# Last layer's experts in seven groups of two and three, and the first group's weights fetched while the mixer still runs

## The chip, the cores and the metric

The kernel runs on one core of one Trainium2 chip. The metric is the device time of one launch in microseconds (us). Three launches of the kernel before took 1733.53, 1736.21 and 1737.06 us; the median, 1736.21 us, is the time before.

## The reference, cut to what matters

The program is a two-layer transformer block followed by a second, different block. Only the end of the first block's last layer matters here: a retention mixer over 512 tokens, a residual, and then a mixture of experts over the last 256 tokens. All is float32.

```python
y, yc = retention_mixer(xm, cm, ret_w_in[idx], ret_w_out[idx], ...)
h = h + g1 * y
xm2 = modulate(rmsnorm(h, norm_g[layer, 1]), sh2, sc2)
f = moe_ffn(xm2.reshape(-1, D), router_w, router_b, moe_w1[layer], moe_w3[layer], moe_w2[layer])
h = h + g2 * f.reshape(h.shape)
...
def moe_ffn(tok, router_w, router_b, w1, w3, w2):
    ...
    for e in range(N_EXPERTS):
        hid = jax.nn.silu(tok @ w1[e]) * (tok @ w3[e])
        out = out + gate[:, e:e + 1] * (hid @ w2[e])
    return out
```

There are 16 experts, each token goes to 2 of them, D is 1024 and the hidden width of an expert is 512. So w1, w3 and w2 of one expert hold 2 MiB each, and all experts of a layer 96 MiB.

## The kernel before, in words

**How the experts are computed.** The kernel doesn't run every token through every expert. It gives each expert a fixed number of rows (a cap) in a group of 128 rows, gathers the chosen tokens into these rows by matmuls with a 0/1 matrix (`gather`, L1382), runs the group through the weights of its experts (`products`, L1403), scales the rows by their gates into `y` (ACT L1451 and DVE L1452) and scatters them back into the accumulator `acc` by matmuls (`scatter`, L1409). `GROUPS[1]` lists the groups of the last layer; `BATCHES` says which groups share one gather. Experts 15 and 14 have fixed places; the fourteen others are ranked on the chip by how many tokens they got, and `(0, 96)` stands for the expert of rank 0 with 96 rows. Where an expert has more tokens than rows, a slow path behind a branch (`overflow`, L1546 to L1548) does the rest.

**What a group costs.** For the 128 rows of a group, `products` makes 24 steps of 512 columns: eight for w1, eight for w3, eight for w2 (four parts of the hidden width, two halves of the output). With several experts in a group the rows are split into column tiles (two of 64, or four of 32) that TensorE works on side by side; each tile reads its own expert's weights.

**How the weights come.** `expert_load` (L192 through `raw`) fetches a piece of 1 MiB, half a matrix, with one DMA on SP's queue; an expert has six pieces, in the order w1, w1, w3, w3, w2, w2. `raw` takes the slots of `self.slots` in turn. `moe_late`, the function of this stage, opens eight slots on the right side of SBUF beside the three that the whole program keeps (`RAW = 3`), so eleven pieces of 8 KiB per partition fit at once. SP works in order: a load whose slot is still being read waits, and all later loads wait behind it. Loads of ranked experts read the expert's number from SBUF first (`values_load` in `places_of`). For the first two groups (`NS = 2`) the loads are issued ahead of the routing (`first`).

**What runs ahead.** `mixer1` is the retention mixer. Its activations `x` (`xact`, 32 KiB per partition) are read by `project(h)` for four heads; `attend(h)` then works on what `project` left in the pool `l1w`. The output projection (`out_T`, eight loads of `ret_w_out`) is interleaved with `attend(3)` and follows it. POOL computes the `rstd` powers (L502) of `attend` in order with its other work.

**Order.** The Tile scheduler sets each engine's order from the code's order, priorities and the pools' releases; a tile in a freed pool waits for the last reader of what lay there.

Of the kernel before, what the change touches and what calls it, by code (L numbers as in the profile page):

```python
# [9 lines left out]
F32 = mybir.dt.float32  # L10
# [8 lines left out]
P = 128  # L19
# [19 lines left out]
NS = 2  # L39
one, two = lambda r: ((r, 128),), lambda a, b: ((a, 64), (b, 64))  # L40
SPLIT = (0, 2, 4, 7, 10, 12)
GROUPS = ((one(15), one(14), one(0), two(8, 13), one(1), one(2), two(9, 12), one(3), one(4), two(10, 11), one(5),
           one(6), one(7)),
          (one(15), one(14), ((0, 96), (13, 32)), ((1, 96), (12, 32)), two(2, 11), two(3, 10), two(4, 9), two(5, 8),
           two(6, 7)))
BATCHES = ((0, 1), (2, 3), (4, 5), (6, 7), (8,))
CAPS = [[dict(x for g in gs for x in g)[r] for r in range(16)] for gs in GROUPS]


# [81 lines left out]
class Kern:  # L131
    def __init__(self, tc, ctx, I, out):
        self.tc, self.nc, self.I, self.out, self.ctx = tc, tc.nc, I, out, ctx
        self.cp = ctx.enter_context(tc.tile_pool(name="const", bufs=1))
        self.sm = ctx.enter_context(tc.tile_pool(name="small", bufs=3))
        self.ps = ctx.enter_context(tc.tile_pool(name="psum", bufs=4, space=PSUM))
        self.nid = 0
        self.aside, self.work = [], []
        self.holds, self.added, self.added_to = [], None, None
        self.slots, self.turn = [], 0  # L140
        ctx.enter_context(self.buffers(RAW))


# [25 lines left out]
    @contextmanager  # L169
    def buffers(self, n, **kw):  # L170

        with self.pool(self.name("raw"), n, **kw) as pool:
            old = self.slots
            self.slots = old + [pool] * n
            yield
            self.slots = old

    @contextmanager
    def splitting(self):
# [390 lines left out]
    def mixer0(self):  # L570
        nc, I, V = self.nc, self.I, self.nc.vector
        W = I["mixab_w_in"][0]
        with ExitStack() as es:
# [147 lines left out]

            Wo, Y = I["mixab_w_out"][0], [[self.psum(tag="g") for _ in range(2)] for _ in range(2)]

            def out_T(c):
                return self.part_T_steps(Y[c], Wo, 0, 256 * c, mx, 0, 512, True, True, (0, 1, 2, 3, 4, 5, 6, 7))

# [7 lines left out]
            for c in range(4):  # L734
                if c > 1:
                    Y.append([self.psum(tag="g") for _ in range(2)])
                    ys.append(out_T(c))
# [48 lines left out]
    def mixer1(self, ss):  # L786
        nc, I, V = self.nc, self.I, self.nc.vector
        W, Wo = I["ret_w_in"][0], I["ret_w_out"][0]
        with ExitStack() as es:
            op = lambda n, b: es.enter_context(self.pool(n, b))  # L790
            lp, wp = op("l1", 1), op("l1w", 2)
            rb = self.stat_end(ss, 0, 512)
            x = self.xact(lp)
            for k in range(KC):
                self.mod_norm(1, rb, x, k)
                self.fill(FT[8 + k])
# [106 lines left out]
            for h in range(3):  # L903
                self.work = [project(h + 1)]
                attend(h)
                self.step(999)
            self.fill(99)
            Y = [self.psum((P, 2, 256), "g") for _ in range(4)]
            self.work = [out_T(0, c) for c in range(4)]
            attend(3)  # L910
            self.step(999)
            for c in range(4):
                self.work = [out_T(8, c)]
                self.step(999)
                if c == 0:
                    ss = self.stat_begin(self.router_begin(1))
                if c == 1:
                    self.router_shift(1)
                for j in range(2):
                    self.residual(1, 2, 2 * c + j, Y[c][:, j], 256)  # L920
                    self.stat_chunk(ss, 2 * c + j, 256, 256)
        return ss


    def router_begin(self, l):
# [362 lines left out]
    def moe_late(self, ss):  # L1288
# [3 lines left out]
        l, n0, NT, N = 1, 256, 2, 256  # L1292
        with ExitStack() as es:
            op = lambda n, b=1: es.enter_context(self.pool(f"{n}{l}", b))
            es.enter_context(self.buffers(8, side="right"))
            rp, wp = op("route"), op("moe", 2)
            order, GR = {}, GROUPS[l]
            load = lambda *a: self.expert_load(l, order, *a)

            def loads(g):  # L1300

                rs = [r for r, _ in GR[g]]
                return [[load(name, r, u, n, c) for r in rs]
                        for name, n, c in (("moe_w1", 8, 512), ("moe_w3", 8, 512), ("moe_w2", 4, 1024)) for u in range(2)]

            first = [loads(g) for g in range(NS)]
            tl, places, gates, rows, nat = self.route(l, ss, rp)
            self.holds = []
            pos, posm = places()
# [18 lines left out]

            cur = batch(BATCHES[0])
            pm, oi, ranked = self.ranking(tl, pos, NT, lambda: tl([NT, 16, 16]))  # L1330
            ranked(place, posm, V)
            rows()
            g, den = gates()
# [17 lines left out]
            def slots(g, oh, a):  # L1351

                ex = GR[g]
                sp = self.psum((P, 2, 4))
                for i, (r, _) in enumerate(ex):
                    for t in range(NT):
                        nc.tensor.matmul(sp[:, i], oh[:, t, a:a + P], pr4[:, r, t, :], start=t == 0, stop=t == NT - 1)
# [2 lines left out]
                for i, (r, n) in enumerate(ex):  # L1360
                    for b in range(a, a + n, 32):

                        c = b + (n if n in (64, 128) else 32)
# [50 lines left out]
            todo = None  # L1414
            for bi, gs in enumerate(BATCHES):
                x, oh, _ = cur
                nxt = batch(BATCHES[bi + 1]) if bi + 1 < len(BATCHES) else None
                chunks = list(range(4)) if nxt else []
                for i, g in enumerate(gs):
                    if g >= NS:  # L1420
                        self.places_of(order, oi, GR[g])
                    ws = loads(g) if g >= NS else first[g]
                    xs = lambda k: x[:, k, P * i:P * i + P]
                    h1 = self.psum()
                    products([h1], xs, ws[0:2], g)
# [28 lines left out]
                    todo = y, back  # L1454
# [622 lines left out]
```

## Time and profile before

| | |
|---|---|
| median of three launches | 1736.21 us |
| the profiled execution | 1734.04 us, span 1732.3 us |
| mean granted TensorE clock of it | 0.976 |
| busy: PE, DVE, ACT, POOL | 94%, 50%, 37%, 15% of the span |
| bytes over the DMA engines | 390 MB, mean 225 GB/s |
| last layer's experts, first to last `products` matmul | 1024.2 to 1280.9 us |

The profile comes from one execution; its own time is 2.2 us below the median of the launches. PE is TensorE's matmul, DVE VectorE, ACT ScalarE, POOL GpSimd; SP issues DMAs. Times in rows are microseconds from the span's start. A PE that is shown busy may still be waiting inside a matmul, so the rows of waits and of DMA traffic are read beside the busy time.

### The profile page before, as it was taken

The numbers are of one execution on the slowest core, as the hardware profiler recorded it, in microseconds if no ns is written. First come the engines' busy times: TensorE is split into PE (matmuls) and PEld (weight loads), VectorE is DVE, ScalarE is ACT, GpSimd is POOL, SyncE is SP. The second block draws the span as 40 slices with busy tenths as digits, with TensorE's granted clock in tenths as the row PEclk, the third lists the DMA queues.
The fourth block names the chain that finished last, engine by engine and source line by source line (L and its number), as shares of the span: only waits on it lengthen the run. The fifth ranks groups of instructions, "written<-read, shape, count | busy, mean of one in ns | idle before, by whom it ended". The sixth has DMA issues, their size and how long they took to land.

```text
span 1732.3 us, 26549 instructions
## 1 busy us (share of the span) xinstructions
PE 1636.9 (94%) x10640; PEld 1222.9 (71%) x10640; DVE 874.4 (50%) x1676; ACT 643.6 (37%) x1008; POOL 266.0 (15%) x265
## 2 busy tenths in 40 slices
PE   5999999988999998999999989999989999999999
PEld 3676657665555455879899955343449999999899
DVE  6565554573424346644555442111135756677665
ACT  3343333333423244433434331010135555655543
POOL 2212101221111111201211020000012110123300
PEclk8999999898999999999999989999989999999999
DMA  9644654477999987354433467999975454433360
GB/s 312 151 134 147 209 187 167 147 311 254 400 384 380 394 326 282 121 194 148 147 122 122 146 252 239 410 420 420 420 257 179 141 159 161 160 122 122 122 214 25
DMA packets 179230, 390.00 MB, mean 225 GB/s; under 512 B 25063, under 2 KB 141864, under 8 KB 149850
## 3 DMA queue, kind: packets, MB, share of 16 engines
q1 hardware_dynamic: 173882, 375.83, 60.1%
q0 software_dynamic: 4336, 10.99, 2.4%
q8 instruction: 87, 1.43, 0.3%
q10 hardware_dynamic: 880, 1.38, 0.2%
q14 instruction: 45, 0.37, 0.1%
HBM read 381.50 MB, written 14.85 MB: 229 GB/s over the span
## 4 chain that ended last, share of the span: by engine, by line
PE 66%; DVE 6%; issue 2%; ACT 2%; POOL 1%; DMA 1%; POOLq 0%; ACTq 0%; DVEq 0%
PE ps L220 12%; PE ps L221 12%; PE ps L222 12%; PE ps L1403 11%; PE ps L1174 8%; PE ps L280 3%; PE ps L1382 1%; DVE wl L211 1%; PE ps L1409 1%; DVE X L1956 1%; PE ps L408 1%; PE ps L1970 1%; DMA w<-in_moe_w_dram 1%; PE ps L1858 0%; PE ps L1839 0%
## 5 line engine op out<-in xcount | busy, mean ns | idle before, releaser
L211 DVE TENSOR_TENSOR wl<-w,wh 128x1024 fp32r<-128x1024 f32 x278 | 346.3, 1261 | 167.3 <-ACT wh L208 165.8
L208 ACT ACTIVATE wh<-w 128x1024 fp32r<-128x1024 f32 x280 | 290.9, 1056 | 200.2 <-PE ps L221 93.1
L220 PE MATMUL ps<-wh,xh 128*128 128x256 f32 x512 | 146.7, 286 | 1.6 <-DVE qk L553 1.6
L221 PE MATMUL ps<-wl,xh 128*128 128x256 f32 x512 | 144.8, 283 | 0.0
L222 PE MATMUL ps<-wh,xl 128*128 128x256 f32 x512 | 144.7, 283 | 0.0
L1403 PE MATMUL ps<-w,xe 128*64 128x512 f32 (+2 forms) x640 | 136.8, 595 | 0.0
L1174 PE MATMUL ps<-w,xe 128*64 128x512 f32 (+1 forms) x320 | 103.6, 596 | 1.2 <-DMA w<-in_moe_w_dram 1.2
L220 PE MATMUL ps<-x,wh 128*128 128x256 f32 x352 | 102.3, 291 | 0.0
L220 PEld LDWEIGHTS ps<-wh,xh 128*128 128x128 f32 x512 | 98.1, 192 | 5.7 <-issue 2.7
L221 PE MATMUL ps<-x,wh 128*128 128x256 f32 x352 | 99.8, 283 | 0.0
L222 PE MATMUL ps<-x,wl 128*128 128x256 f32 x352 | 99.8, 283 | 0.0
L221 PEld LDWEIGHTS ps<-wl,xh 128*128 128x128 f32 x512 | 98.2, 192 | 0.2
L222 PEld LDWEIGHTS ps<-wh,xl 128*128 128x128 f32 x512 | 98.2, 192 | 0.0
L1403 PEld LDWEIGHTS ps<-w,xe 128*64 128x64 f32 (+2 forms) x640 | 43.4, 131 | 72.9 <-issue 70.4
L220 PE MATMUL ps<-xh,wh 128*128 128x512 f32 (+1 forms) x224 | 83.2, 380 | 3.4 <-ACT xh L541 3.0
L221 PE MATMUL ps<-xl,wh 128*128 128x512 f32 (+1 forms) x224 | 82.7, 371 | 1.6 <-DVE xl L542 1.1
L222 PE MATMUL ps<-xh,wl 128*128 128x512 f32 (+1 forms) x224 | 81.4, 364 | 0.9 <-DVE wl L211 0.9
L1174 PEld LDWEIGHTS ps<-w,xe 128*64 128x64 f32 (+1 forms) x320 | 38.3, 158 | 57.5 <-issue 54.6
L220 PEld LDWEIGHTS ps<-x,wh 128*128 128x128 f32 x352 | 67.1, 191 | 1.4
L221 PEld LDWEIGHTS ps<-x,wh 128*128 128x128 f32 x352 | 67.3, 191 | 1.2 <-issue 0.2
L220 PE MATMUL ps<-wh,xp 128*128 128x256 f32 x224 | 65.5, 292 | 2.3 <-ACT xp L1659 2.3
L222 PEld LDWEIGHTS ps<-x,wl 128*128 128x128 f32 x352 | 67.2, 191 | 0.4
(472 smaller groups left out, 3669.8 us busy)
## 6 DMA issues: line engine op xcount, KB each, us to landing
w<-in_moe_w_dram SPq DMA_DIRECT2D x192, 1024.0 KB, 11.6
w<-in_w_in_dram SPq DMA_DIRECT2D x48, 1024.0 KB, 5.0
w<-in_ada_w_dram SPq DMA_DIRECT2D x40, 1024.0 KB, 5.1
w<-in_ret_w_in_dram SPq DMA_DIRECT2D x24, 1024.0 KB, 5.2
w<-in_mixab_w_in_dram SPq DMA_DIRECT2D x10, 1024.0 KB, 6.2
w<-in_ada_w_dram SPq DMA_DIRECT2D x16, 512.0 KB, 8.4
w<-in_ret_w_out_dram SPq DMA_DIRECT2D x8, 1024.0 KB, 5.1
w<-in_mixab_w_out_dram SPq DMA_DIRECT2D x4, 1024.0 KB, 7.4
```

Source lines behind the costliest of these rows:

```text
L208: nc.scalar.activation(hi, t[:, b:b + hk], AF.Copy)
L211: eng.tensor_tensor(out=lo, in0=t[:, b:b + hk], in1=hi.bitcast(F32), op=OP.subtract)
L220: mm(ps, lh, rh, start=start, stop=False, skip_group_check=skip)
L221: mm(ps, lh, rl, start=False, stop=False, skip_group_check=skip)
L222: mm(ps, ll, rh, start=False, stop=stop, skip_group_check=skip)
L280: self.nc.tensor.transpose(out, in_, self.ident[:n, :n])
L408: nc.tensor.matmul(ps[32 * j:32 * j + 32, :], self.S[:, kc, :], w[:, j * 512:(j + 1) * 512], start=kc == 0, stop=kc == KC - 1)
L1174: nc.tensor.matmul(ps[a], x[0][:, q, a], t[:, k, s], start=first, stop=last)
L1382: nc.tensor.matmul(ps[:, j, 0:w], nat[i % 2][:, i // 2, k * P:(k + 1) * P], oh[:, i // 2, 0:w], start=i == 0, stop=i == 2 * NT - 1)
L1403: nc.tensor.matmul(ps[a:b], lhs(u * m + k)[:, a:b], we[e][:, k, 512 * c:512 * c + 512], start=u == k == 0, stop=u == len(ws) - 1 and k == ...
L1409: nc.tensor.matmul(acc[k // 2][:, k % 2], y[i][:, k * P:(k + 1) * P], back, start=start and k % 2 == i == 0, stop=stop and i == 1, skip_gr ...
L1956: mul = lambda e, o, i1: e.tensor_tensor(out=o, in0=o, in1=i1, op=OP.mult)
```

## The change

The last layer gets seven groups in place of nine: experts 15 and 14 share one (64 rows each, 128 each before), rank 0 shares with rank 13 as before, ranks 1 and 2 have 64 rows each in groups of three with two experts of 32 rows, and ranks 3 to 8 are in pairs. The caps of ranks 9, 10 and 11 fall from 64 to 32, that of rank 1 from 96 to 64. The first group is a batch of its own.

The eight right-hand slots are no longer opened by `moe_late`. `x` of the mixer moves into a pool of its own on the right side, which is closed after `project(3)`; there `ahead(4, ...)` opens four slots and issues the four w1 pieces of experts 15 and 14 on POOL's queue. After `attend(3)` the pool `l1w` is closed and the four w3 pieces follow in the same way. `moe_late` takes these eight slots over (`joined`); of the first group only the four w2 pieces are left to SP, and all later groups load when their turn comes.

```diff
-          (one(15), one(14), ((0, 96), (13, 32)), ((1, 96), (12, 32)), two(2, 11), two(3, 10), two(4, 9), two(5, 8),
-           two(6, 7)))
-BATCHES = ((0, 1), (2, 3), (4, 5), (6, 7), (8,))
+          (two(15, 14), ((0, 96), (13, 32)), ((1, 64), (12, 32), (11, 32)), ((2, 64), (10, 32), (9, 32)), two(3, 8),
+           two(4, 7), two(5, 6)))
+FIRST = [(e, name, u) for name in ("moe_w1", "moe_w3") for u in range(2) for e in (15, 14)]
+BATCHES = ((0,), (1, 2), (3, 4), (5, 6))
...
+    @contextmanager
+    def joined(self):
+
+        old, self.slots, self.turn = self.slots, self.slots + self.later, 0
+        yield
+        self.slots = old
...
+            own, tmp = es.enter_context(ExitStack()), es.enter_context(ExitStack())
+            wp = tmp.enter_context(self.pool("l1w", 2))
-            x = self.xact(lp)
+            x = self.xact(own.enter_context(self.pool("l1x", 1, side="right")))
...
             self.fill(99)
+            own.close()
+            first = iter(FIRST)
+            self.first = self.ahead(4, first)
             Y = [self.psum((P, 2, 256), "g") for _ in range(4)]
             self.work = [out_T(0, c) for c in range(4)]
             attend(3)
             self.step(999)
+            tmp.close()
+            self.first += self.ahead(4, first)
...
+    def ahead(self, n, todo):
+
+        pool = self.late.enter_context(self.pool(self.name("raw"), n, side="right"))
+        self.later += [pool] * n
+        ts = []
+        for e, name, u in islice(todo, n):
+            ...
+            self.nc.gpsimd.dma_start(out=t, in_=src[:, u * k // 2:(u + 1) * k // 2, :])
+            ts.append(t)
+        return ts
...
-            es.enter_context(self.buffers(8, side="right"))
+            es.enter_context(self.late)
+            es.enter_context(self.joined())
...
-                return [[load(name, r, u, n, c) for r in rs]
+                done = iter(self.first if g == 0 else ())
+                return [[next(done, None) or load(name, r, u, n, c) for r in rs]
...
-            first = [loads(g) for g in range(NS)]
+            first = loads(0)
```

The first place is POOL's queue around `attend(3)`. Before, the two `rstd` powers of `attend(3)` (tiles `st`) follow the decay tables of head 3 directly, and the sums of squares (`sq`) come next:

```order
L848 AFFINE_SELECT dtmp_1299_7794<-dtmp_1299_7794 128x256
L850 TENSOR_TENSOR dec_1260_7568<-dec_1260_7568,dtmp_1299_7794 128x256
L502 TENSOR_TENSOR st_1343_8234<-st_1343_8234,mhalf_89 128x1
L502 TENSOR_TENSOR st_1346_8253<-st_1346_8253,mhalf_89 128x1
L475 TENSOR_TENSOR sq_1370_8532<-sq_1370_8532,sq_1371_8537 128x256
```

Now (`w` are the weight tiles) four loads stand ahead of the two powers and four, with two small ones for the next block's bias, ahead of the sums:

```order
L949 DMA w_1327_8153<-in_moe_w1_dram 128x2048
L949 DMA w_1328_8155<-in_moe_w1_dram 128x2048
L949 DMA w_1329_8157<-in_moe_w1_dram 128x2048
L949 DMA w_1330_8159<-in_moe_w1_dram 128x2048
L511 TENSOR_TENSOR st_1348_8249<-st_1348_8249,mhalf_89 128x1
L511 TENSOR_TENSOR st_1351_8268<-st_1351_8268,mhalf_89 128x1
L949 DMA w_1370_8489<-in_moe_w3_dram 128x2048
L949 DMA w_1371_8491<-in_moe_w3_dram 128x2048
L949 DMA w_1372_8493<-in_moe_w3_dram 128x2048
L949 DMA w_1373_8495<-in_moe_w3_dram 128x2048
L1774 DMA relb_9837<-in_rel_bias_2_dram 32x24
L484 TENSOR_TENSOR sq_1380_8559<-sq_1380_8559,sq_1381_8564 128x256
```

Two groups of four loads are new on POOL; the work behind them is the same.

The second place is SP's queue where the experts' loads begin. Before, the last load of the mixer (`ret_w_out`) is followed by twelve loads of experts 15 and 14; these are the first three and the last, and then the overflow count `cnti` and the branch:

```order
L192 DMA w_1389_8698<-in_ret_w_out_dram 128x8x256
L192 DMA w_1404_8796<-in_moe_w1_dram 128x2048
L192 DMA w_1405_8798<-in_moe_w3_dram 128x2048
L192 DMA w_1406_8800<-in_moe_w3_dram 128x2048
...
L192 DMA w_1408_8804<-in_moe_w2_dram 128x2048
L1546 TENSOR_LOAD cnti_1515_9211
L1546 ISA x2
L1548 COMPARE_AND_BRANCH
```

Now there are three loads, the count, a fourth load, and then the ranked loads of the second group (`order` holds the experts' numbers), the first and last of which are shown, ahead of the branch:

```order
L201 DMA w_1399_8725<-in_ret_w_out_dram 128x8x256
L201 DMA w_1406_8805<-in_moe_w2_dram 128x2048
L201 DMA w_1407_8807<-in_moe_w2_dram 128x2048
L201 DMA w_1408_8809<-in_moe_w2_dram 128x2048
L1577 TENSOR_LOAD cnti_1532_9386
L1577 ISA x2
L201 DMA w_1409_8811<-in_moe_w2_dram 128x2048
L1513 TENSOR_LOAD order_1441_8891
L201 ISA
L201 DMA w_1498_9186<-in_moe_w1_dram 128x2048
...
L201 DMA w_1509_9208<-in_moe_w2_dram 128x2048
L1579 COMPARE_AND_BRANCH
```

Eight loads left SP's queue, and the branch moved from behind the twelfth piece to behind the twenty-fourth.

## Rows read from the trace of the kernel before

**Rows 1.** The page's slices of 43.3 us: PE's busy tenths and the DMA rate.

```profile
PE   5999999988999998999999989999989999999999
...
GB/s 312 151 134 147 209 187 167 147 311 254 400 384 380 394 326 282 121 194 148 147 122 122 146 252 239 410 420 420 420 257 179 141 159 161 160 122 122 122 214 25
```

**Rows 2.** Windows: routing, then groups 0 to 3 and 5 to 8.

```profile
core 0: us, PE busy (x) PEld busy (x) DVE busy (x) ACT busy (x) POOL busy (x), PEclk, DMA share, GB/s
1002.00:1024.20 22.20, 14.14 (x71) 10.90 (x70) 17.90 (x64) 10.20 (x23) 7.51 (x11) 0.62 0.96 381
1024.20:1048.30 24.10, 23.36 (x72) 11.81 (x71) 5.03 (x20) 3.59 (x5) 1.23 (x4) 1.00 0.59 203
1048.30:1076.30 28.00, 27.65 (x105) 15.52 (x104) 7.00 (x29) 3.88 (x7) 0.00 (x0) 1.00 0.77 255
1076.30:1107.60 31.30, 30.18 (x231) 10.75 (x230) 5.36 (x15) 3.17 (x5) 0.57 (x1) 1.00 0.87 352
1107.60:1136.50 28.90, 27.77 (x233) 11.28 (x232) 5.37 (x20) 3.17 (x5) 0.56 (x1) 1.00 1.01 410
...
1165.50:1194.50 29.00, 27.87 (x137) 12.24 (x136) 4.40 (x14) 3.17 (x5) 0.00 (x0) 1.00 1.01 420
1194.50:1224.60 30.10, 28.97 (x138) 12.36 (x137) 3.63 (x10) 2.95 (x5) 0.00 (x0) 1.00 1.01 420
1224.60:1254.60 30.00, 28.86 (x138) 12.29 (x137) 3.63 (x10) 2.95 (x5) 0.00 (x0) 1.00 1.01 420
1254.60:1283.60 29.00, 27.12 (x132) 11.57 (x131) 4.43 (x13) 3.37 (x7) 1.22 (x4) 1.00 0.81 311
```

**Rows 3.** Chain that ended last, through group 5: start, us, what.

```profile
1165.60 1.00 PE ps L1403 x2
1166.60 1.14 PE ps L1382 x8
...
1168.70 7.02 PE ps L1403 x32
...
1176.25 7.02 PE ps L1403 x30
...
1185.81 6.22 PE ps L1403 x28
```

**Rows 4.** Timeline of PE at the stage's end: start, us, what.

```profile
1279.41 1.45 PE L1403 MATMUL ps<-w,hh 128*64 128x512 f32 x5
```

**Rows 5.** SP: waits from 1027 to 1262 (us, times, longest), and timeline at 1026.

```profile
SPq L192 <- PE ps L1403: 188.8, 64, 20.8
...
SPq L1548 <- SPq L1548: 4.2, 2, 3.7
...
1027.83 8.15 SPq L192 DMA_DIRECT2D w<-in_moe_w_dram  x3
```

**Rows 6.** DMA issues: count, KB each, median us from issue to landing.

```profile
w<-in_ret_w_out_dram SPq DMA_DIRECT2D x8, 1024.0 KB, 5.1
...
bD<-bD POOLq DMA_DIRECT2D x1, 1536.0 KB, 9.5
```

**Rows 7.** Window around that bD copy.

```profile
1104.00:1119.00 15.00, 14.72 (x114) 6.29 (x113) 2.11 (x6) 2.57 (x4) 0.56 (x1) 1.00 1.02 412
```

**Rows 8.** Timeline of POOL from 940 to 1012.

```profile
951.84 0.55 POOL L502 TENSOR_TENSOR st<-st,mhalf 128x1 f32<-128x1 f32 x1 [34.08 <-DVE st L501]
...
1002.31 0.66 POOL L1743 DMA_DIRECT2D relb<-in_rel_bias_dram  x1 [2.15 <-PE ps L222]
```

**Rows 9.** Timelines of PE, SP and ACT at the mixer's end.

```profile
942.06 0.28 PE L222 MATMUL ps<-wh,xl 128*128 128x256 f32 x1
...
957.44 0.60 PE L280 MATMUL ps<-c_main,ru 128*128 128x128 f32 x4
...
958.77 12.68 SPq L192 DMA_DIRECT2D w<-in_ret_w_out_dram  x3
...
971.62 1.06 ACT L208 ACTIVATE wh<-w 128x1024 fp32r<-128x1024 f32 x1 [1.82 <-PE ps L221]
```

More of the change, by code (lines that the diff above doesn't have):

```diff
@@ L140, in __init__ @@
         self.slots, self.turn = [], 0
+        self.late, self.later = ExitStack(), []
         ctx.enter_context(self.buffers(RAW))
@@ L790, in mixer1 @@
             op = lambda n, b: es.enter_context(self.pool(n, b))
-            lp, wp = op("l1", 1), op("l1w", 2)
+            lp = op("l1", 1)
+            own, tmp = es.enter_context(ExitStack()), es.enter_context(ExitStack())
+            wp = tmp.enter_context(self.pool("l1w", 2))
             rb = self.stat_end(ss, 0, 512)
-            x = self.xact(lp)
+            x = self.xact(own.enter_context(self.pool("l1x", 1, side="right")))
             for k in range(KC):
@@ L922, in mixer1 @@
         return ss
+    def ahead(self, n, todo):
[3 more added lines that the diff above has]
+        for e, name, u in islice(todo, n):
+            k, c = (4, 1024) if name == "moe_w2" else (8, 512)
+            t = pool.tile([P, 2048 // c, c], F32, tag="w", name=self.name("w"))
+            src = self.I[name][1, e:e + 1].rearrange("o (p k) c -> p (o k) c", k=k)
+            self.nc.gpsimd.dma_start(out=t, in_=src[:, u * k // 2:(u + 1) * k // 2, :])
+            ts.append(t)
+        return ts
     def router_begin(self, l):
@@ L1353, in slots @@
                 ex = GR[g]
-                sp = self.psum((P, 2, 4))
+                sp = self.psum((P, 3, 4))
                 for i, (r, _) in enumerate(ex):
@@ L1419, in moe_late @@
                 for i, g in enumerate(gs):
-                    if g >= NS:
+                    if g:
                         self.places_of(order, oi, GR[g])
-                    ws = loads(g) if g >= NS else first[g]
+                    ws = loads(g) if g else first
                     xs = lambda k: x[:, k, P * i:P * i + P]
```

## The prediction

> **What bounds the kernel now.** Read the slices first [rows 1]: PE is busy nearly everywhere, and from slice 26 to 29 the DMA rate stands at 410 to 420 GB/s, the highest of the span. That is the last layer's experts, so two resources are full at once there, and the question is which of them ends the stage. The windows by group [rows 2] answer it. Groups 5 to 7 take 29.0, 30.1 and 30.0 us, with PE busy for all but 1.1 us of each; groups 0 and 1 take 24.1 and 28.0 us at 203 and 255 GB/s. A group costs 24 to 31 us whether the DMA engines are idle or full, so PE sets the pace. The chain through group 5 [rows 3] says of what: four pieces of `products` (1.00 + 7.02 + 7.02 + 6.22 = 21.3 us), two gathers (the first 1.14), scatters and short waits for DVE and ACT. SP confirms it: its loads wait 188.8 us for the matmuls that read the slots [rows 5]. Loads wait for PE, PE not for loads.
>
> The two are nearly balanced, though. A pair needs twelve pieces of 1 MiB, 12.58 MB, which take 30.0 us at the 420 GB/s of [rows 2]; PE needs 29. The 96 pieces, 100.7 MB, take 240 us at that rate, and nine groups took 1024.2 to 1280.9 [rows 4], 256.7 us.
>
> **The change: the groups.** Two groups fewer save PE two times 29 us. Column tiles run side by side, so two, three or four experts cost a group the same 21.3 us: group 3 (four tiles, 28.9 us by the table's times, 1107.6 to 1136.5) and group 5 (two tiles, 29.0) agree. PE alone would now need: group 0 24.1 us plus two more gathers of 1.14 [rows 2, 3], 26.4; six more at 29, less two gathers in each of the last two (4.6), plus 2.3 for the bias matmuls that made group 2 take 31.3. That is 198 us, an end at 1222.
>
> But the groups don't share bytes. A group of three needs 18 pieces: 18.87 MB, 44.9 us at 420 GB/s, where PE needs 29. So the loads become the bound, and the sum goes by their stream:
>
> - It starts where the first slot comes free. Eleven pieces fit in both programs, and all stand there at 1024.2: before, they arrive during the routing (22.2 us at 381 GB/s is 8.5 MB, eight pieces [rows 2]); now eight arrive earlier and the engines idle in that stretch. **So I credit the early fetch with nothing by itself.** Either way the twelfth piece waits for the first half of w1 of group 0, and SP issued it at 1027.83 [rows 5]. Bytes flow some 2.6 us later (5.1 us from issue to landing of a single load [rows 6], less 2.5 for its bytes): 1030.4.
> - 85 pieces are left, 89.1 MB: 212.2 us at 420 GB/s, 1242.6. The slots allow it: with eleven, piece n waits for piece n-11 to be read, 27 us of stream earlier, while PE follows within a few us of landing.
> - The copy of `bD` (1536 KB [rows 6]) passes through the same engines in this stage. Before it took bytes from a stream that had a lead; now it is on the path: 1.57 MB, 3.7 us; its window shows the total rate unchanged at 412 GB/s [rows 7].
> - At the start few loads are in flight. The bounds: nothing, or the 352 GB/s of group 2 for the first 30 us of stream (5 us; the 255 of group 1, where loads come one by one, would make it 12). Group 0 now frees slots in twos, so I am nearer to nothing: 2 us.
> - The last landing is then at 1248.3; PE still runs half of w2 (a third of 21.3, halved: 3.6): 1251.9, against 1280.9 before. **29 us less.**
>
> Most of PE's new idle time lies in the second group of three and at the end of the first, in waits of about 4 us (7.5 us of stream for three pieces, 3.5 us of matmuls). In the pairs that follow PE (29, later 27 us) keeps up with the stream (30).
>
> A rule speaks against this sum. The Trainium skill, "DMA: Bandwidth & Descriptors", Specifications, gives about 358 GB/s as a core's share of HBM. The trace disagrees: three groups ran at 420 [rows 2]. By 358 the 89.1 MB would take 249 us, and the total would come out 37 us later than I forecast.
>
> **The change: the mixer's end.** The last matmul that reads `x` starts at 942.06, and the last transposes of `attend(3)` end at 958.04 [rows 9]; at these two points POOL issues four loads each. A load costs POOL 0.66 us to issue [rows 8], 2.6 us for four; the next power is due at 951.84, nine us later, and the sums of squares after 980, so nothing behind them is late. If a POOL load took three times as long, eight us, it would still fit. The four loads are 4.19 MB, 10 us at 420 GB/s. The second four start beside the sixth `ret_w_out` load, issued at 958.77 [rows 9]. Alone it lands after 5.1 us, at 963.9, and its split begins at 971.62, so 7.7 us are spare; sharing the engines evenly would delay it by 2.5. I cost this end at nothing, with 5 us as the upper bound if loads queued behind each other. `x` on the right side, and the local reordering at the mixer's start, move the same work: nothing, within 2 us either way.
>
> SP's branch now sits behind the second group's loads. It cost about 4 us there before [rows 5]. Then the DMA queue still holds three pieces, so it costs nothing; without that cover, 4 us.
>
> **The sum.** The profiled execution took 1734.0 us; less 29 is 1705.0. The median of launches was 2.2 us above that execution, so I predict 1707. A difference of 0.2%, 3.5 us, is about what a measurement of this kernel can tell from no change.
>
> **The rivals.**
>
> - *The stream runs short.* If 89.1 MB flow at the 352 GB/s of group 2 [rows 2], they take 253 us, 41 more: 1748, slower than before. The point from which it decides is 89.1 MB in 241 us, 370 GB/s; near it nothing changes. For it: PE now waits, and SP's waits may break the queue. Against it: groups 5 to 7 held 420, and loads queue deeper when PE waits. Chance 0.08, half of it slower, half near no change.
> - *PE's clock falls while it waits.* In the routing, PE was busy for 14.1 of 22.2 us and the granted clock was 0.62 of 2.4 GHz on the mean; in the group after it 1.00 [rows 2]. At 1.2 GHz a step of three pieces takes 7 us, just inside the stream's 7.5, so the groups of three hide it. A pair would take 29 + 21 = 50 us against 30. If the first pair after the threes runs so, 20 us are lost and the next two win 3 each back: 1721, chance 0.10. If all three pairs run so, 60 us: 1767, slower; it decides from one and a half pairs at the lower level. Chance 0.03, since the clock returned within one stretch above. The Trainium skill, "TensorE: Matmul & The Clock Gate", on oscillation in real kernels, describes just this: waits for DMA between tiles, and every next tile at the lower clock. Half-fed pairs are not in this trace; group 8 at 311 GB/s kept 1.00.
> - *The mixer's end pays.* The early loads hold up `ret_w_out` and POOL by 10 us in all: 1717, chance 0.05.
> - *It doesn't do what it says.* With smaller caps a group could overflow into the slow path: sixteen experts, 96 MB again one half-piece after another; at the 203 GB/s of group 0 that is over 490 us more. By the reference's routing of the given inputs, experts 15 and 14 get 24 and 40 tokens (64 rows), and ranks 0 to 13 get 73, 64, 45, 44, 39, 33, 23, 23, 20, 20, 17, 17, 17, 13. All fit, but rank 1 has 64 in 64 rows. Chance 0.02.
>
> **Chances and range.** The forecast has 0.72. Faster: 0.72 + 0.10 + 0.05 = 0.87; same 0.04; slower 0.04 + 0.03 + 0.02 = 0.09. Low end: no early loss, the copy hidden, 2 us won by reordering and 2 of scatter between medians: 1697. High end: the clock rival's 1721 with the 5 us of early loss: 1727, which takes in the mixer rival too.
>
> **What would show it.** Right: the windows between 1030 and 1250 at about 420 GB/s throughout, PE waiting for `w` in the two groups of three, the last `products` near 1252, and the shift first appearing inside the experts' stage, with the mixer's end unmoved at 1002. Wrong: the same stage with a rate under 400 or a granted clock under 1 in the pairs; a `ret_w_out` split later than before; or a stage that starts later than 1024.

## The result, and the profile after

The changed kernel takes 1710.82 us (median of four launches, 1709.54 to 1713.53); the kernel before, launched beside it, 1734.87. The ratio is 0.9864, with a 95% interval of 0.9844 to 0.9883: some 24 us less. Forecast were 1707.0 us and a range of 1697 to 1727, so the time lies in the range and 3.8 us above the number. The profiled execution took 1709.54 us, its span is 1707.5.

The slices of the page, now of 42.7 us, answer to [rows 1]. The lines are PE's busy tenths, the granted clock in tenths, and the DMA rate:

```profile
PE   5999999988999998999999989789979999999999
...
PEclk9999999898999999899999979899989999999999
...
GB/s 319 151 136 149 210 173 188 149 288 260 400 379 386 393 359 266 135 200 124 173 131 123 341 26 360 384 415 420 420 262 185 150 166 149 171 124 122 118 206 26
```

Counted from 1 as in the prediction, slice 23 (341 GB/s) holds the early pieces, and slice 24, the routing, now moves almost nothing (26). From slice 25 to 29 the rate is 360 to 420. PE's busy tenths show 7 and 8 in slices 26 and 27, in the midst of the stage; before, PE had no such gap there.

The windows by group of the changed kernel, cut where `products` of the next group begin, answer to [rows 2]. The first line is the whole stage, from the first to the last `products` matmul, then come groups 0 to 6:

```profile
core 0: us, PE busy (x) PEld busy (x) DVE busy (x) ACT busy (x) POOL busy (x), PEclk, DMA share, GB/s
1018.54:1257.03 238.49, 210.06 (x1220) 83.28 (x1219) 31.52 (x112) 20.97 (x34) 2.71 (x8) 0.96 0.95 389
1018.54:1047.36 28.82, 28.82 (x141) 12.13 (x144) 5.90 (x29) 3.17 (x6) 0.35 (x2) 0.91 0.75 305
1047.29:1087.13 39.84, 29.94 (x251) 14.29 (x249) 6.48 (x24) 3.85 (x6) 0.00 (x0) 0.89 0.92 377
1087.13:1130.63 43.50, 39.70 (x285) 14.47 (x284) 6.29 (x22) 3.76 (x6) 1.14 (x2) 0.98 0.94 377
1130.63:1168.64 38.01, 30.97 (x183) 9.67 (x183) 4.06 (x11) 2.57 (x4) 0.00 (x0) 0.96 1.01 421
1168.64:1198.57 29.93, 28.45 (x138) 12.00 (x137) 3.90 (x10) 3.17 (x5) 0.00 (x0) 1.00 1.01 420
1198.57:1228.73 30.16, 26.81 (x121) 10.81 (x120) 3.21 (x9) 2.57 (x4) 0.00 (x0) 1.00 1.01 420
1228.73:1257.03 28.30, 25.45 (x114) 9.98 (x113) 1.76 (x8) 1.88 (x3) 1.22 (x4) 1.00 1.02 405
```

Read the last column first. From group 3 on the rate is 405 to 421 GB/s and a pair takes 28 to 30 us, as many as its twelve pieces need. In groups 0 to 2 it is 305, 377 and 377: that is where the stage loses time. Before, the stage took 256.7 us (1024.18 to 1280.86); now 238.5. That is 18.2 of the 24.8 us by which the two spans differ; 5.6 more lie ahead of the stage, 1.0 behind it.

Finer windows, ten microseconds each, show how the rate was lost (the first is the stage's start):

```profile
1015.00:1025.00 10.00, 10.00 (x35) 5.38 (x37) 4.99 (x21) 1.67 (x2) 2.25 (x5) 0.56 0.01 2
...
1045.00:1055.00 10.00, 10.00 (x82) 3.27 (x79) 1.50 (x2) 1.92 (x3) 0.00 (x0) 1.00 1.01 418
1055.00:1065.00 10.00, 10.00 (x90) 4.84 (x89) 1.03 (x6) 0.65 (x2) 0.00 (x0) 1.00 0.67 250
1065.00:1075.00 10.00, 8.51 (x76) 3.27 (x76) 3.81 (x17) 1.97 (x3) 0.00 (x0) 1.00 1.01 425
1075.00:1085.00 10.00, 1.58 (x7) 1.59 (x8) 0.15 (x1) 0.00 (x0) 0.00 (x0) 0.67 1.01 417
1085.00:1095.00 10.00, 10.00 (x71) 4.66 (x73) 0.00 (x0) 0.60 (x1) 0.00 (x0) 0.82 0.70 261
```

Two holes: 250 and 261 GB/s where 420 would flow, each (420 - 250 or 261) / 420 x 10 = about 4 us of bytes. Two engines stand shortly ahead of them, and both at the same instruction: the branch to the slow path (`overflow`, L1579 here). These are its instructions on each engine, with count, shortest, median and longest duration in ns, first and last start, and who waited for it:

```profile
L1579 SPq EVENT_SEMAPHORE  x8: 17/17/17, 1056.9 to 1060.9; - x8
L1579 SPq COMPARE_BRANCH  x1: 53/53/53, 1051.7 to 1051.7; - x1
L1579 PEldq COMPARE_BRANCH  x1: 6012/6012/6012, 1071.2 to 1071.2; - x1
...
  PE ps L1440: 9.9, 1
```

SP reaches the branch at 1051.7, behind its load of 1050.98, and issues the next load only at 1061.55; between them stand eight semaphore events. PE's sequencer takes 6.0 us for the compare and branch, and the matmuls behind it (`scatter`) start 9.9 us after the last one ahead:

```profile
1071.62 1.90 PE L1434 MATMUL ps<-w,hh 128*32 128x512 f32 x16
1083.41 3.78 PE L1440 MATMUL ps<-back,y 128*128 128x256 f32 x16 [9.90 <-issue]
1087.13 1.79 PE L1434 MATMUL ps<-w,xe 128*32 128x512 f32 x4
```

While PE stands it frees no slots. SP's waits for slots from 1060 to 1100 (us, times, longest) show what follows, 18.1 us without an issue, from 1074.1 to 1092.8, and the second hole:

```profile
SPq L201 <- PE ps L1434: 26.3, 6, 18.1
```

That was the theory to test: **the stage is bound by the stream of weights, and the stream is broken twice at the branch.** The rivals: PE still sets the pace (seven slower groups); or the early transfers themselves bring the gain.

### The profile page after: what moved, and what is told of

Same layout as the page of the kernel before. It is cut to its first block, busy times and chain, and to the rows that moved or that the text cites. A ratio compares the mean times of both kernels' runs of the same rounds, so it can differ in the third digit from the quotient of the medians.

```text
span 1707.5 us, 26393 instructions
## 1 busy us (share of the span) xinstructions
PE 1593.7 (93%) x10568; PEld 1194.4 (70%) x10568; DVE 866.8 (51%) x1658; ACT 636.6 (37%) x998; POOL 270.1 (16%) x273
## 5 line engine op out<-in xcount | busy, mean ns | idle before, releaser
L1434 PE MATMUL ps<-w,xe 128*32 128x512 f32 (+1 forms) x640 | 115.5, 618 | 10.4 <-DMA w<-in_moe_w_dram 10.3
L1434 PEld LDWEIGHTS ps<-w,xe 128*32 128x32 f32 (+1 forms) x640 | 31.7, 125 | 79.4 <-issue 57.0
L573 ACT ACTIVATE p<-ps,st 128x512 f32<-128x512 f32 (+1 forms) x64 | 38.5, 605 | 76.2 <-DVE st L570 69.7
```

Source lines behind the costliest of these rows:

```text
L573: nc.scalar.activation(p[:, 0:w], S, AF.Exp, bias=st[:, 0:1], scale=1.0, accum_out=st[:, 1:2])
L1434: nc.tensor.matmul(ps[a:b], lhs(u * m + k)[:, a:b], we[e][:, k, 512 * c:512 * c + 512], start=u == k == 0, stop=u == len(ws) - 1 and k == ...
```

## The experiments

All times stand in one table, the stage and the way to it from each run's trace ("to the stage" is the time from the first matmul of the mixer's norm, `ps<-ones,sq`, to the first `products`; "stage" from there to the last). Runs with one number in the first column ran side by side on one chip, with the same launches of the kernel before.

| set | kernel | median us | ratio to before (95%) | to the stage | stage |
|---|---|---|---|---|---|
| 0 | before | 1734.87 | 1 | 341.3 | 256.7 |
| 0 | changed | 1710.82 | 0.9864 (0.9844 to 0.9883) | 338.7 | 238.5 |
| 1 | groups alone | 1715.60 | 0.9893 (0.9864 to 0.9923) | 342.8 | 238.6 |
| 1 | early fetch alone | 1729.77 | 0.9982 (0.9967 to 0.9996) | 338.0 | 256.6 |
| 1 | branch behind group 4 | 1707.80 | 0.9852 (0.9822 to 0.9881) | 338.7 | 235.3 |
| 1 | half of the loads | 1673.23 | 0.9657 (0.9620 to 0.9695) | 338.1 | 198.4 |
| 2 | changed again | 1711.05 | 0.9873 (0.9856 to 0.9889) | 338.5 | 238.5 |
| 2 | no branch | 1705.25 | 0.9846 (0.9830 to 0.9862) | 337.6 | 230.8 |
| 2 | pools moved, early loads on SP | 1709.65 | 0.9861 (0.9842 to 0.9880) | 338.7 | 239.4 |
| 2 | branch last, copy in the routing, ninth slot | 1711.71 | 0.9875 (0.9848 to 0.9902) | 346.7 | 224.1 |
| 3 | copy in the mixer | 1705.86 | 0.9837 (0.9819 to 0.9854) | 340.3 | 230.0 |
| 3 | and a ninth slot | 1706.33 | 0.9841 (0.9827 to 0.9854) | 340.1 | 227.9 |
| 3 | and the branch behind group 4 | 1703.43 | 0.9827 (0.9809 to 0.9846) | 340.1 | 229.4 |
| 4 | code shifted | 1709.03 | 0.9858 (0.9835 to 0.9881) | 338.6 | 233.8 |

Launches of one kernel differ by 3 to 9 us, so effects of 2 to 5 us are read from the two columns on the right, which repeat far better: the changed kernel gave 238.49 us for the stage both times.

### What bounds the stage

Half of the loads were left out, with the same work for PE:

```diff
+                out = []
+                for name, n, c in (("moe_w1", 8, 512), ("moe_w3", 8, 512), ("moe_w2", 4, 1024)):
+                    for u in range(2):
+                        out.append(out[-1] if u and g else [next(done, None) or load(name, r, u, n, c) for r in rs])
+                return out
```

> The changed kernel with the second half of every matrix not loaded from group 1 on; the matmuls read the first half twice, so the result is another, but TensorE's work is the same. Theory (stream): TensorE alone needs about 198 us for the stage by the prediction's sum, plus its stall at the branch, so the stage takes 200 to 212 us in place of 238.5 and the time is 1673 to 1685. Rival (TensorE sets the pace): the stage stays within 5 us of 238.5 and the time within 1706 to 1713.

The stage took 198.4 us (the prediction's sum for PE alone was 198), the time 1673.23. These 198.4 us still hold 7.1 us in which PE stood at the branch. So PE could do the seven groups 40 us faster, and what holds them in the changed kernel is the loads. In this run PE waited for no load at all behind group 1; in the changed kernel it waited 11.5 us for them by the rows, and more inside matmuls that are shown as busy (the same 1220 matmuls are busy for 210 us there and 189 here). The waits of PE over groups 2 to 6 of the changed kernel (line, us in total, times, longest), and the stage of the run with half the loads:

```profile
PE ps L1434 <- DMA w<-in_moe_w_dram: 11.5, 11, 1.9
```

```profile
1019.84:1218.26 198.42, 188.94 (x1220) 78.53 (x1219) 31.35 (x112) 20.92 (x34) 2.65 (x8) 0.97 0.66 248
```

### The two parts of the change, each alone

Groups alone: the kernel before with the new `GROUPS` and `BATCHES`, `first = loads(0)` and a PSUM tile for three experts; mixer and slots as before.

> The seven groups without the early fetch: the mixer, x and the eight slots are as before, and SP loads the first eleven pieces of experts 15 and 14. Theory (stream): eleven pieces stand ready when the first products start either way, so the stage of the last layer's experts takes the same 238.5 us as in the changed kernel, and the time is 1711, within 4 us. Rival (early fetch pays): the 5.7 us by which this stage starts earlier in the changed kernel (1018.5 against 1024.2) come from the early fetch and the moved x; then this run starts the stage at 1024 and takes 1716 to 1718.

The stage took 238.6 us, as in the changed kernel, so the first half of the expectation holds to 0.1 us. The time, 1715.6 us, fits the rival's number better: the way to the stage is 4.1 us longer than in the changed kernel.

Early fetch alone: the changed kernel with the nine groups of before.

```diff
-FIRST = [(e, name, u) for name in ("moe_w1", "moe_w3") for u in range(2) for e in (15, 14)]
+FIRST = [(e, name, u) for e in (15, 14) for name in ("moe_w1", "moe_w3", "moe_w2") for u in range(2)][0:8]
...
-                done = iter(self.first if g == 0 else ())
+                done = self.done if g < NS else iter(())
```

> The early fetch without the seven groups: the nine groups of before, the eight early pieces being the six of expert 15 and two of expert 14. Theory (stream): the nine groups are bound by TensorE, the queue has a lead, and eleven pieces stand ready either way, so the time is that of before, 1735, within 4 us. Rival (early fetch pays): 1729 or less.

Between the two: 1729.77, a ratio of 0.9982 (0.9967 to 0.9996). The stage is unchanged (256.6 us), as the stream theory says, but the way to it is 3.3 us shorter. Something ahead of the stage does pay. One run kept the moved pools and emptied the list of early pieces:

```diff
-FIRST = [(e, name, u) for name in ("moe_w1", "moe_w3") for u in range(2) for e in (15, 14)]
+FIRST = []
```

> The changed kernel with an empty list of early pieces: pools and groups as changed, but SP loads all twelve pieces of experts 15 and 14, eleven of them before the first products. Theory (stream): eleven pieces stand ready either way, so the time is within 2 us of the changed kernel, 1711. Rival (the early transfers themselves pay, by a routing stage free of traffic or otherwise): 4 us or more slower than the changed kernel, 1715.

It is as fast as the changed kernel run beside it (0.9861 against 0.9873), with the same 338.7 us to the stage and a stage of 239.4. But it does not test the early transfers. Its slots stand open as early as in the changed kernel, so SP itself fetches eleven pieces between 938 and 987, and the routing moves nothing there either. Its DMA issues from 935 to 1000 (count, KB each, median us to landing) and its window of the routing:

```profile
w<-in_moe_w_dram SPq DMA_DIRECT2D x11, 1024.0 KB, 8.6
```

```profile
1000.00:1020.00 20.00, 13.54 (x60) 10.49 (x61) 17.11 (x62) 9.63 (x21) 6.90 (x10) 0.54 0.00 0
```

It shows only that the queue, POOL's or SP's, makes no difference beyond 1 us. The two runs above and the place of the gain do separate the parts. In the stage the early transfers are worth 0.1 us: 238.6 us without them and 238.5 with them for seven groups, 256.7 and 256.6 us for nine. Ahead of the stage the gain comes before 936.5, when the first early piece is issued. From the start of the mixer to the first `wh,xh` matmul (the same 112 matmuls) the kernel before takes 28.9 us and the changed one 26.7; two waits of PE for DVE are gone, 1.2 of these 2.2 us, which the kernel before shows as

```profile
696.98 0.39 PE L221 MATMUL ps<-xl,wh 128*128 128x256 f32 x1 [0.35 <-DVE xl L534]
700.19 0.73 PE L222 MATMUL ps<-xh,wl 128*128 128x512 f32 x2 [0.88 <-DVE wl L211]
```

The projections behind them (1696 matmuls) take 230.6 and 229.7 us. The rest, from there to the first `products`, holds the early transfers: 82.9 us in the groups alone and 82.3 in the changed kernel, and with nine groups 81.8 before and 81.7 with the early fetch. **So the early transfers are worth at most 1 us, and the moved pools some 3** (28.9 - 26.7 and 230.6 - 229.7). Which of the moves it is, `x` on the right side or the earlier end of `l1w`, was not separated.

The matmuls that read `x` run a little faster, as one of three such groups of 384 shows (busy us, mean ns of one), of the kernel before (700 to 950) and of the changed one (695 to 945):

```profile
L220 PE MATMUL ps<-wh,xh 128*128 128x256 f32 x384 | 108.9, 284 | 0.0
```

```profile
L229 PE MATMUL ps<-wh,xh 128*128 128x256 f32 x384 | 108.2, 282 | 0.7 <-DVE rt L828 0.7
```

On the mean these 1152 matmuls start 118.3 ns apart here and 119.9 before, which makes 1.8 us; a wait for DVE of 0.7 us, seen in the second row, takes part of it back. For these matmuls only the places of tiles differ. Why an address should matter was not tried.

### The branch

First the changed kernel again, beside the next runs:

> The changed kernel as it is, beside the next three on one chip. Both theories: about 1711, with a stage of 238.5 us and rates of 250 and 261 GB/s in the ten microseconds after SP's and TensorE's stall at the branch.

It repeats: 1711.05 us, stage 238.49, rates of 247 and 280 GB/s where the first profile has 250 and 261. Then without the branch, by leaving out the call of `overflow`:

> The changed kernel without the slow path and its branch (left out: the handling of experts with more tokens than rows, of which the given inputs have none). Theory (the branch empties the load queue): SP stands at the branch until every load that it has issued has landed, TensorE stands for the code behind it, and each hole costs 4 us of bytes: 7 to 8 us less than the changed kernel, 1703, a stage of 231, no ten microseconds under 400 GB/s between 1035 and 1245. Rival (the holes have another cause, such as slots freed late by TensorE): they stay, and the time stays within 2 us of the changed kernel.

The stage takes 230.8 us, 7.7 less, and the time 1705.25, 5.8 less than the changed kernel beside it. At the places of the two holes the rate is now

```profile
1055.00:1065.00 10.00, 10.00 (x92) 5.59 (x88) 2.64 (x10) 0.60 (x1) 0.00 (x0) 1.00 1.01 417
...
1085.00:1095.00 10.00, 8.03 (x59) 3.02 (x54) 1.39 (x5) 0.60 (x1) 0.00 (x0) 1.00 1.01 418
```

Both holes belong to the branch. Moving it does only half:

```diff
-                    if g == 1:
+                    if g == 4:
                         c4 = lambda a: a.rearrange("p (k c) -> p k c", c=P)
```

> The changed kernel with the branch to the slow path called behind group 4 in place of group 1. Theory (stalls at the branch empty the load queue): in the changed kernel SP stands 10.2 us and TensorE 9.9 us at this branch while the queue is short, and the rate falls to 250 and 261 GB/s in the ten microseconds after each, about 4 us of bytes each time. Behind group 4 eight pieces (20 us) are queued, so neither stall empties it: 7 to 8 us less, 1703. Rival (TensorE sets the pace of the seven groups): its 9.9 us are lost wherever the branch stands, and the time stays at 1711.

1707.80 us and a stage of 235.3: 3.2 us won where 7 to 8 were expected. The idea that eight queued pieces would cover SP's wait was wrong, and this trace says why best: SP's waits from 1169 to 1190, its instructions at the branch, and the time from issue to landing of the load ahead of it, issued at 1169.34:

```profile
SPq L1579 <- SPq L1579: 18.9, 8, 3.1
```

```profile
L1579 SPq EVENT_SEMAPHORE  x8: 17/17/17, 1170.6 to 1188.6; - x8
```

```profile
w<-in_moe_w_dram SPq DMA_DIRECT2D x1, 1024.0 KB, 19.3
```

Eight events follow each other over 18.9 us, about 2.5 us apart, the landing spacing of a piece; the last comes at 1188.6, when the last load has landed (1169.34 + 19.3). In the changed kernel it is the same with fewer loads in flight (9.9 us from the issue at 1050.98, the last event at 1060.9). SP thus waits at the branch until **every load it has issued has landed**, however many there are. A longer queue makes the wait longer, and the hole behind it, from the last landing to the next bytes, stays: 231 GB/s here between 1185 and 1195. Before the change the same branch stood 4.2 us [rows 5] in a stage that had loads to spare.

### The code behind the branch, and the copy

The bias set-up with its `bD` copy was moved from group 2 to the mixer's end, the copy issued by SP:

```diff
             tmp.close()
+            bp = op("bias", 1)
...
+                if c == 2:
+                    self.bias_setup(bp)
...
-                    if g == 2:
-                        with self.pool("bias", 1) as bp:
-                            self.bias_setup(bp)
...
-        nc.gpsimd.dma_start(out=bD, in_=bvs)
+        nc.sync.dma_start(out=bD, in_=bvs)
...
-        nc.gpsimd.dma_start(out=self.bD2, in_=bass.AP(tensor=bD[:, :].tensor, offset=bD[:, :].offset, ap=[[0, 64], [1, 6144]]))
+        nc.sync.dma_start(out=self.bD2, in_=bass.AP(tensor=bD[:, :].tensor, offset=bD[:, :].offset, ap=[[0, 64], [1, 6144]]))
```

> The changed kernel with the bias set up at the mixer's end, and the bD copy issued by SP behind the three w2 loads that it has there, in place of inside group 2. Theory (stream): 1.57 MB leave the stage's stream, and the copy lies where the DMA engines are idle: the stage takes 3.7 us less than the 238.5 of the changed kernel, 234.8, and the time is 1707. Rival (the copy was hidden in the stage, or costs as much at its new place): within 1.5 us of the changed kernel, 1710 or more.

1705.86 us, and a stage of 230.0: 8.5 less, more than twice what the copy's bytes explain. The trace had the second cause: PE stood 4.1 us behind the branch, not 9.9, and the hole at 1085 was gone. In the changed kernel two packets of the instruction queue, 16 KB each, come while PE stands there (1071 to 1084):

```profile
q1 hardware_dynamic: 741, 5.42, 100.5%
q8 instruction: 2, 0.03, 1.0%
```

So code is fetched by the same engines that are 100% busy with weights. The two packets begin at 1074.7 and 1080.9; the branch ends 2.5 us after the first (1077.2) and the matmuls start 2.5 us after the second (1083.4), so PE waited for two in a row. With the bias moved, the branch ends 2.5 us after a packet of 1075.9, and the matmuls follow 0.3 us later. The explanation to test was that moving the bias's matmuls ahead had shifted the code. To test that alone, the changed kernel got four idle matmuls at the mixer's end:

```diff
+                if c == 2:
+                    pad = self.psum()
+                    for _ in range(4):
+                        nc.tensor.matmul(pad[0:8, 0:128], self.ident[:, 0:8], self.ident, start=True, stop=True)
```

> The changed kernel with four small matmuls (128 columns, nothing reads their sum) added at the mixer's end, which only moves TensorE's later code by a few instructions. In the kernel with the copy in the mixer the stage was 8.5 us shorter in place of 3.7, and TensorE stood 4.1 us behind the branch in place of 9.9. Theory (a second block of code): in the changed kernel the code behind the branch runs into the next 16 KB block after two instructions, and that block is fetched behind the queued weights, 5.8 us more; shifted, the place behind the branch needs one fetch: TensorE stands 4 to 5 us, the hole of 261 GB/s at 1085 goes, the stage takes 234 to 235 us, the time is 1707. Rival (the 4.8 us came with the copy, by its bytes or by POOL's and TensorE's part of it inside group 2): TensorE stands 9 to 11 us again, the stage stays at 238.5 and the time at 1711.

PE stood 5.0 us, one packet of code came in that time (1073.9 to 1081.4), the hole at 1085 was gone (417 GB/s), and the stage took 233.8 us, 4.7 less than in the changed kernel. About 1.0 of these 4.7 is not the branch's: in this trace the first slot came free 5.3 us after the stage began, in the changed kernel 6.3, with a granted clock of 0.84 in the first ten us against 0.74. The timeline of PE, and the windows that answer to the two holes:

```profile
1081.33 3.75 PE L1444 MATMUL ps<-back,y 128*128 128x256 f32 x16 [5.04 <-PEq L1583]
```

```profile
q8 instruction: 1, 0.02, 0.9%
```

```profile
1055.00:1065.00 10.00, 10.00 (x92) 3.37 (x84) 0.00 (x0) 1.20 (x2) 0.00 (x0) 1.00 0.69 286
...
1085.00:1095.00 10.00, 10.00 (x77) 3.23 (x76) 0.00 (x0) 0.60 (x1) 0.00 (x0) 0.90 1.01 417
```

The launches (1709.03, 0.9858) don't separate this from the changed kernel; the stage does. The copy itself is then the rest: 233.8 - 230.0 = 3.8 us, where the prediction had 3.7. This is a difference of two single traces whose hole at SP's stop is not the same either, so it is good to about 1 us.

### More slots, and the branch at other places

A ninth slot, with the first half of w2 of expert 15 fetched ahead as well:

```diff
-FIRST = [(e, name, u) for name in ("moe_w1", "moe_w3") for u in range(2) for e in (15, 14)]
+FIRST = [(e, name, u) for name in ("moe_w1", "moe_w3", "moe_w2") for u in range(2) for e in (15, 14)]
...
-            self.first += self.ahead(4, first)
+            self.first += self.ahead(5, first)
```

(Two temporaries of `overflow` move to a single-buffered pool to make room.)

> The kernel with the copy in the mixer, and besides a ninth slot with a ninth piece (the first half of w2 of expert 15) fetched ahead, so that all twelve pieces of group 0 stand ready. Theory (stream): one piece less in the stream, 2.5 us, a stage of 232.3 us, 1704.5. Rival (the early pieces don't matter, since TensorE's start sets when slots free): the stage stays at 234.8.

The stage fell by 2.0 us (2.5 expected), to 227.9, though the first slot came free 0.45 us later than in the run before; the launches don't show it (1706.33 against 1705.86).

> Both of these, and the branch behind group 4 in place of group 1, which alone took 3.2 us off the stage. Theory (stream, and one hole in place of two): a stage of 229 us, 1701.5; the one hole of some 4 us stands where SP waits at the branch for its loads to land. Rival (the three edits hide each other): a stage of 232 us or more, 1704 or more.

This was a miss for the stage: 229.4, 1.5 more than with the branch at group 1. With one packet of code, PE's wait at group 1 no longer costs bytes, so only SP's hole was left to move, and it costs no less at the new place: 220 and 392 GB/s between 1175 and 1195, 5.4 us of bytes at 420, against 274 and 371 between 1055 and 1075 with the ninth slot alone, 4.6 us. The time is the lowest of all, 1703.43, 0.9827 (0.9809 to 0.9846), though its interval overlaps with the two above it.

> Three edits that the stream theory prices: the branch behind the last group (both holes gone, 8 us, less 2 us for TensorE's wait at the end), the bD copy before the routing (its 1.57 MB leave the stream, 3.7 us), and a ninth slot with a ninth piece fetched ahead (2.5 us). Theory (stream): 12 us less than the changed kernel, 1699, a stage of 224 to 227 us. Rival (the rate of the queue or TensorE's single steps limit the stage): less than 5 us gained, 1706 or more.

Here the stage did what was expected, 224.1 us without a hole, and the time did not: 1711.71. With the bias set up at the start of the routing, the way to the stage took 346.7 us, 8.2 more than in the changed kernel beside it; PE stood 6.7 us for a tile of the routing that DVE makes. And the branch at the end cost 7 us behind the stage: the first large matmul of the next block came 20.5 us after the last `products`, against 13.5 in the changed kernel, of which PE stood 3.5 us at the branch, and the small matmuls behind took 2.5 us more (32 in 6.82 us against 4.36). The timeline of PE at its end:

```profile
1257.29 3.75 PE L1441 MATMUL ps<-back,y 128*128 128x256 f32 x16 [3.47 <-PEq L1578]
1260.84 6.82 PE L502 MATMUL ps<-cols,sq 128*128 128x2 f32 x32
```

## Why the prediction was right, and where it was not

**Right: what binds.** Seven groups need 198 us of PE by the prediction, and 198.4 were measured; the stage then runs at the loads' rate. That the two numbers agree so closely is luck: the measured stage holds 7.1 us of standing at the branch and 2.1 of a low clock at its start (w1 of group 0 in 9.17 us, w3 in 7.09), of which the sum had neither, so its groups were some 9 us too long. PE's waits for loads were also shorter than the 4 us that it expected: eleven, 1.9 us at most. The pairs take 28 to 30 us at 405 to 420 GB/s, and the rival of a stream at 352 GB/s fell. The Trainium skill, "HBM Reference", Specifications (TRN2), says of a core that streams alone that it gets about 425 GB/s, and of 358 as its share with both cores streaming. The trace agrees with the first, 420 to 421 in groups 3 to 5, and the prediction had weighed only the second.

**Right: the early fetch credited with nothing by itself.** The stage takes 238.6 us with the groups alone and 238.5 with the early fetch, and the way to it differs by 0.6 us where the transfers run. What the prediction called "nothing, within 2 us either way" for `x` and the reordering was wrong in size: some 3 us, and all of it ahead of the early pieces.

**Right: the copy of bD**, 3.7 us forecast, 3.8 by the difference of two runs.

**Wrong: the branch.** The step reads "the DMA queue still holds three pieces, so it costs nothing; without that cover, 4 us". The cover doesn't exist, since SP leaves the branch only when the queue is empty. By the windows the holes cost 4.0 us behind SP's stop and 3.8 behind PE's, 7.8 together. Taking the branch out won 7.7 us and shifting the code 4.7, with 0.4 to 1.0 us in each from an earlier first slot (5.6 and 5.3 us after the stage began, 6.0 and 6.3 in the two traces of the changed kernel). For SP's part the runs with the ninth slot give 3.9 (227.9 with the branch at group 1, 224.1 with it behind the last group, where no expert's loads follow; they differ also in the place of the bias set-up). PE's part was in no term: in [rows 2] group 1 ended without a gap there. Against 7.8 us for both holes the sum had 2 us of early loss, and its second price, "4 us" without cover, is about what SP's hole alone cost.

**Wrong: the start.** The first `products` began at half the clock (granted clock 0.56 from 1015 to 1025, back at the full clock from 1023.8): w1 of group 0 took 9.68 us, where w3 took 7.09. So the first slot came free 6.3 us after the stage began (1024.82), not 3.6: 2.7 us. The sum had taken the 3.6 from a kernel whose first `products` ran at the full clock. The lower clock came with the groups, not with the early fetch: these are the first ten us of the stage with the groups alone and with the early fetch alone (the third number from the end is the clock), and then the first w1 and w3 of the changed kernel:

```profile
1026.04:1036.04 10.00, 10.00 (x36) 3.18 (x36) 1.40 (x9) 0.35 (x2) 0.30 (x2) 0.74 0.28 86
```

```profile
1018.71:1028.71 10.00, 10.00 (x32) 4.97 (x31) 2.88 (x13) 2.36 (x3) 0.76 (x3) 1.00 0.33 107
```

```profile
1018.54 9.68 PE L1434 MATMUL ps<-w,xe 128*64 128x512 f32 x32
...
1029.29 7.09 PE L1434 MATMUL ps<-w,xe 128*64 128x512 f32 x32
```

Together: the stage was to take 227.7 us and took 238.5. Holes of 7.8 less 2, and the start's 2.7, explain 8.5 of the 10.8 us. The missing 2.3 us are open; the change of rate around the copy (384 GB/s from 1125 to 1135) may be 0.9 of them. On the other side 5.6 us were won ahead of the stage: 2.6 in the mixer and routing of this trace (341.3 to 338.7), and 3.0 before the mixer, where the program is the same in both; there the mixer's start lies anywhere from 679.4 to 683.9 us over the fourteen traces, so that part is chance. And 1.0 behind the stage. That is 10.8 - 5.6 - 1.0 = 4.2 us less won than forecast, 1705.0 + 4.2 = 1709.2 for the profiled execution; it took 1709.54. So the error of 10.8 us in the stage was larger than the final difference tells, and that the forecast came so close is partly luck. One of its own signs of being wrong had come in, windows under 400 GB/s in the stage, and one of its signs of being right had not: the shift begins ahead of the stage. (The range's upper end is a slip too: 1721 and 5 us make 1726, not 1727.)

**The clock rival** did not decide. In the three pairs at the end the granted clock stayed at 1.00, and in the groups of three at 0.96 to 0.98. It fell to 1.2 GHz for 10.2 us when PE stood at the branch (0.67 and 0.82 in the windows from 1075 to 1095), and for 3.4 us from 1133.0, in the second group of three, after waits for loads of 1.9 and 1.5 us. In the run without the branch it also fell once in the last pair, for 3.4 us from 1239.4. None of this lasted as the rival needs.

## What to carry to other kernels

When an edit moves a stage from PE's bound to the loads' bound, look again at everything that was free before: a branch, a copy, a fetch of code. Here each of them took bytes from the stream or stopped an engine that feeds it, and each cost 3 to 5 us. Leaving half of the loads out is a cheap test of which side binds: here it gave PE's own 198 us, its stop at the branch included.

The branch on the engine that issues the loads emptied its queue, with some four loads in flight or with eight. No place tried for it was free: behind group 4 the hole stayed, and behind the last group 7 us came in behind the stage. And judge effects of a few microseconds on the length of their own stage, since whole launches hide them.

## What the runs showed of the hardware

- TensorE's code is fetched while the program runs, in packets of 16 KB over the DMA engines. With these full of weights PE's compare and branch took 6.0 to 7.0 us, with half of the loads left out 3.3. With the engines full PE stood 9.7 to 10.7 us where it waited for two packets in a row (four traces), 4.1 to 5.0 us with one (three traces). Four idle matmuls far ahead of the branch decided which.
- The mixer's 256-column matmuls started 118.3 ns apart on the mean in each of the twelve traces with `x` on the right side of SBUF, and 119.9 in the two with it on the left; 1152 of them make 1.8 us. Why is open.
- SP's stop at the branch grew with its queue: its last semaphore event came 9.9 us after the issue of the last load where that load took 9.9 us to land, and 19.3 us after it where it took 19.3.
